# Projections of queries and keys in groups of four token tiles, their squares summed on ScalarE, and the ninth tile moved into the attention

## The chip, the cores and the metric

The kernel runs on one core of one Trainium2 chip. The metric is the device time of one execution in microseconds, the median of three runs. Engines are named as the profile names them: PE is TensorE's matmul stream and PEld its weight loads, DVE is VectorE, ACT is ScalarE, POOL is GpSimd, SP is SyncE, which issues the DMAs here (its queue is SPq).

## The reference

One inference step of one decoder layer for 1024 prompt tokens and 32 sample tokens (8 sequences of 4), width 1024. Three residual sub-layers: a mixer with two parallel branches, a cross-attention into 256 memory tokens, and a gated feed-forward network. The change touches the mixer alone:

```python
u, v, cq, ckv, kpe = split_in(rms_norm(xp, g_mix) @ w_in)     # 512, 512, 256, 256, 32 columns
a_out = gelu(u) * chunk_gmlp(v)                                # branch A, chunks of 128 tokens
ckv_n = rms_norm(ckv, g_kv_a)                                  # also an output
q = rms_norm((rms_norm(cq, g_q_a) @ w_uq), g_qk_q)             # 8 heads x 96, norm per head, rope on 32
k = rms_norm(concat([ckv_n @ w_uk, kpe]), g_qk_k)              # 8 heads x (64 + 32), norm per head, rope
vv = ckv_n @ w_uv                                              # 8 heads x 64
b_out = softmax(causal(q @ k.T * 96**-0.5)) @ vv               # branch B
xp = xp + concat([rms_norm(a_out), rms_norm(b_out)]) @ w_o
```

The sample tokens go through the same projections, but attend over 4096 cached tokens each, read from pages.

## The kernel before

Tokens are cut into nine tiles: eight of 128 prompt tokens and a ninth of the 32 sample tokens. For the projections from the input they are also cut into three chunks (`CH`) of 384, 384 and 288 tokens. Every large product is made of three matmuls (`mm3`, line 186) over operands that are split into a rounded high part (ACT, lines 192 and 196) and the rest as a low part (DVE, lines 193 and 199).

Order of the work: outside of the stretches marked `manual_schedule` the framework orders each engine's instructions by a planner of its own; inside them the listed engines keep the order of the program. Pools are regions of SBUF. All tiles of one tag in a pool share that tag's slots, and a tile waits for the tiles whose memory it takes over.

`phase1` loads the transposed input in six raw tiles of the tag `xr` (three chunks, two halves of the rows), written by `xload` on SP in program order, and splits them into `xh` and `xl`. The rows of x, needed for the squares that give each token's scale `rs_tok`, come by `tload`: tiles 0 to 2 into `xt`, tiles 3 to 8 into the memory of `a_all`, a later result, which takes over the memory of the raw tiles' pool `px`. The first product, with `w_v0`, is evacuated from five PSUM banks (`mm`) by a GELU with that scale (line 426). Further products give branch A in `a_all`. Then the chunk loop (line 506) makes the latents: cq into `cqh`, `cql`, ckv into `ckr`; sums of squares by matmuls with ones (`tok_sums`), an inverse square root on DVE of 13 small instructions (`rsqrt`, lines 221 to 232), the scale spread over the partitions by `tok_bc` (a diagonal matrix on DVE, line 275, and a matmul), the scaling (line 543), and the split into `ckh`, `ckl`. Behind each chunk `mix` normalises, transposes and stores two tiles of branch A: tiles 0 to 3, 4 to 7, and 8 behind the last chunk.

`phase2a` makes the rope tables (line 574, DVE), and for the first four heads (`hf` 0) projects q, k and v in `proj_group`, in groups of two tiles and the ninth alone. `part` evacuates q with a copy, squares it on ACT in one pass (line 791) and sums per head on DVE (line 792); for k it squares head by head with ACT's accumulator (line 789). `norm` makes the inverse square roots of a group, turns the rope part of q on POOL (lines 562 to 565), and scales k on DVE (814) and POOL (815). `head_prep` transposes a head's q and k (line 838). The second half's weights are loaded and split by `proj_weights`.

Then comes the attention, in a manual schedule: units of a head and two query tiles, 32 in order, worked off in 82 steps. Other work is put into the steps by hand, in `extra`, with `spread(fs, t0, t1)`: transposes of later heads, the second half's projections (`late`), and from step 41 on the preparation of the sample tokens. The stages behind (pages, output projection, memory attention, feed-forward network) are not touched.

Of the kernel before, what the change touches and what calls it, by code (L numbers as in the profile page):

```python
# [155 lines left out]
class Net:  # L156
# [111 lines left out]
    def tok_bc(self, p, ps, r, c):  # L268

        nc = self.nc  # L270
        o, n = CH[c]
        for i, (t0, tn) in enumerate(TILES):
            if o <= t0 < o + n:
                dg = self.t(p, [P, P], F32, "diag", 2)[:tn, :tn]
                nc.vector.tensor_scalar(dg, self.ident[:tn, :tn], r[:tn, i : i + 1], None, ALU.mult)
                nc.tensor.matmul(ps[:, t0 - o : t0 - o + tn], self.ones[:tn], dg, start=True, stop=True)


    def phase1(self):
# [25 lines left out]
        def xload(c, e):  # L305
            o, n = CH[c]
            xrs.append(self.t(px, [P, 4, 384], F32, "xr", 6)[:, :, :n])
            nc.sync.dma_start(xrs[-1], I["xT"][:, 4 * e : 4 * e + 4, o : o + n])
# [197 lines left out]
        for c, (o, n) in enumerate(CH):  # L506
# [31 lines left out]
            nc.vector.tensor_copy(self.sq_tok[:, ct], t[:, :, 0])  # L538
            nc.vector.tensor_copy(ck_tok[:, ct], t[:, :, 1])
            t = self.t(pp, [P, 512], F32, "st", 3)[:, :n]  # L540
            self.tok_bc(pl, t, ck_tok, c)
# [8 lines left out]
            for i0 in ((0, 2), (4, 6), (8,))[c]:  # L550
# [16 lines left out]
    def rope_tables(self, p, cos, sin, g, name):  # L567
# [3 lines left out]
        for nm, t in (("c", cos), ("s", sin)):  # L571
            o = p[nm] if isinstance(p, dict) else self.t(p, [P, 9, 2, 16], F32, f"{name}_{nm}")
            for h in range(2):
                nc.vector.tensor_tensor(
# [5 lines left out]
    def phase2a(self):  # L580
# [50 lines left out]
        groups = ((0, 2), (2, 4), (4, 6), (6, 8), (8, 9))  # L631
        for g in groups:
# [8 lines left out]
        st.append({**heads(), **self.proj_weights((pm, [P, 512], F32, "pth", 5), 1)})  # L641
# [16 lines left out]
        for (q, _), t in zip(late, ((16, 20), (18, 23), (21, 26), (24, 29))):  # L658
            spread(q, *t)
        spread(self.head_prep(pm, pp, 4, st[1], c), 29, 33)  # L660
        spread(sum([v for _, v in late], []) + late[4][0], 28, 38)
# [5 lines left out]
        with tc.manual_schedule(engines={E.PE, E.Activation, E.DVE}):  # L667
# [15 lines left out]
            def mix(G):  # L683
# [5 lines left out]
                nt = lambda j: self.t(p, [P, 2, 4, 96], F32, "k", 4).rearrange("p m h d -> p (m h d)")[:, :512]  # L689
# [57 lines left out]
    def proj_weights(self, raws, hf):  # L747

        nc, I, s = self.nc, self.I, {}
        for nm, src, n in (("q", I["w_uq"], 384), ("v", I["w_uv"], 256)):  # L750
            hi, lo = (self.t(self.lat, [P, 2, n], FR, f"w{nm}{x}") for x in "hl")
            for k in range(2):
                raw = self.t(*raws)[:, :n]
                nc.sync.dma_start(raw, src[:, k, hf * n : hf * n + n])
                self.split(hi[:, k], lo[:, k], raw)
# [5 lines left out]
    def proj_group(self, p, pp, hf, i0, i1, s, c, tt=("tp", 4)):  # L761
# [5 lines left out]
        def alloc():  # L767
            nonlocal r, kk, q
            r = self.t(p, [P, 2, 2, 4], F32, "hr", 2)[:tn, :m]
            kk = self.t(p, [P, 2, 4, 96], F32, "k", 4)[:tn, :m] if i0 < 8 else None  # L770
            q = self.t(p, [P, 2, 4, 96], F32, "q", 4)[:tn, :m] if i0 < 8 else self.qs[:, hf * 4 : hf * 4 + 4].unsqueeze(1)

        def part(i, z):
# [12 lines left out]
            sq = self.t(p, [P, 4, n // 4], F32, f"hsq{z}")[:tn]  # L786
            if z == 1:
                for j in range(4):
# [1347 lines left out]
```

## Time and profile before

| | us |
|---|---|
| median of the three runs | 1956.38 (1953.4 to 1957.37) |
| profiled execution | 1957.17 |
| its span | 1955.4 |
| PE busy | 1875.0 |
| DVE busy | 1358.3 |
| ACT busy | 900.5 |
| POOL busy | 680.8 |

The time is a little more than the span, by what lies around the first and last instruction. A view of stretches gives for each stretch its length, then the busy time of PE, PEld, DVE, ACT and POOL with their instructions in brackets, then the granted clock of TensorE, DMA's share and GB/s. Matmuls are pipelined, so a busy PE is not PE at its peak. A row of the timeline is start, duration, engine, line, operation, out<-in with shapes, and in square brackets how long the engine had been idle and what released it; durations of neighbours overlap, so costs of a sequence are read from start to start. A row of waits is engine and line, what it waited for, the total, how often, and the longest. The page's table of slices and its groups by line were read too; the lines that matter stand in the prediction.

### The profile page before, as it was taken

How to read it: one execution, taken by the hardware profiler on the slowest of the kernel's cores; microseconds unless marked ns; L12 is line 12 of the kernel's file. 1: busy time of each engine (PE TensorE's matmuls, PEld its weight loads, DVE VectorE, ACT ScalarE, POOL GpSimd, SP SyncE). 2: the span in 40 equal slices, each digit the busy share in tenths (PEclk: the TensorE clock that was granted, in tenths of full speed). 3: DMA queues.
4: the chain of work that ended last, by engine and by line, in shares of the span. 5: the costliest groups of instructions: out<-in, count | busy, mean ns of one | idle time of the engine just before them, and what ended most of it. 6: DMA issues, size and time to landing. Idle time of an engine off the chain costs nothing.

```text
span 1955.4 us, 40099 instructions
## 1 busy us (share of the span) xinstructions
PE 1875.0 (96%) x14538; PEld 1764.2 (90%) x14538; DVE 1358.3 (69%) x2963; ACT 900.5 (46%) x1874; POOL 680.8 (35%) x789
## 2 busy tenths in 40 slices
PE   6999899999999999999999988899999999999999
PEld 6999677769888998988799978899999999999999
DVE  7756867767777766776644659888888888832421
ACT  6335667665555555555432546332333323421311
POOL 1221311003544444544032016467677775100000
PEclk9999899999999999999999999999999999999999
DMA  8102000107765566653655045122222222754642
GB/s 294 47 18 71 22 2 34 42 21 213 213 180 167 163 174 177 173 171 128 191 155 182 23 164 180 33 77 91 74 77 68 87 88 77 221 170 127 198 123 66
DMA packets 131513, 233.75 MB, mean 120 GB/s; under 512 B 20594, under 2 KB 86995, under 8 KB 131315
## 3 DMA queue, kind: packets, MB, share of 16 engines
q1 hardware_dynamic: 130450, 230.14, 38.8%
q8 instruction: 115, 1.88, 0.4%
q10 hardware_dynamic: 864, 1.05, 0.1%
q14 instruction: 84, 0.68, 0.1%
HBM read 199.46 MB, written 31.66 MB: 118 GB/s over the span
## 4 chain that ended last, share of the span: by engine, by line
PE 68%; DVE 8%; issue 5%; DMA 4%; POOL 2%; ACT 1%; SPq 1%; POOLq 0%; DVEq 0%; ACTq 0%
PE s L186 15%; PE d L186 13%; PE X L186 7%; PE b L186 6%; PE F L186 6%; PE E L186 6%; PE A L186 3%; PE o L896 2%; PE tp L883 2%; PE o L1326 1%; PE tp L186 1%; DVE mx L1277 1%; POOL S L1274 1%; PE tp L838 1%; DVE y L1846 1%
## 5 line engine op out<-in xcount | busy, mean ns | idle before, releaser
L186 PE MATMUL s<-w2h,ch 128*128 128x288 f32 (+1 forms) x1024 | 305.9, 299 | 0.0
L186 PE MATMUL s<-w2h,cl 128*128 128x288 f32 (+1 forms) x1024 | 295.1, 288 | 2.0 <-POOL cl L1213 2.0
L186 PE MATMUL s<-w2l,ch 128*128 128x288 f32 (+1 forms) x1024 | 294.6, 288 | 0.0
L186 PE MATMUL d<-a,hi 128*128 128x264 f32 x1408 | 261.5, 287 | 3.6 <-ACT a L192 2.0
L186 PEld LDWEIGHTS d<-a,hi 128*128 128x128 f32 x1408 | 220.8, 190 | 4.8 <-DVE a L193 2.5
L186 PEld LDWEIGHTS s<-w2h,ch 128*128 128x128 f32 x1024 | 192.6, 188 | 19.1 <-issue 13.6
L186 PE MATMUL d<-a,lo 128*128 128x264 f32 x704 | 201.2, 286 | 0.0
L186 PEld LDWEIGHTS s<-w2h,cl 128*128 128x128 f32 x1024 | 192.4, 188 | 2.5 <-POOL cl L1213 2.3
L186 PEld LDWEIGHTS s<-w2l,ch 128*128 128x128 f32 x1024 | 192.8, 188 | 0.0
L1256 DVE TENSOR_REDUCE ss<-sq 128x16 f32<-128x1024 f32 x128 | 155.5, 1215 | 47.0 <-ACT sq L1253 46.8
L193 DVE TENSOR_TENSOR lo<-raw,hi 128x1024 fp32r<-128x1024 f32 (+1 forms) x71 | 82.7, 1167 | 136.2 <-ACT hi L192 136.2
L192 ACT CAST hi<-raw 128x1024 fp32r<-128x1024 f32 (+1 forms) x71 | 71.0, 1000 | 185.7 <-PE d L186 157.0
L1213 POOL TENSOR_TENSOR cl<-cT,ch 128x512 fp32r<-128x512 f32 x64 | 83.5, 1304 | 166.8 <-ACT ch L1209 145.2
L186 PEld LDWEIGHTS d<-a,lo 128*128 128x128 f32 x704 | 133.9, 190 | 0.0
L1253 ACT ACTIVATE sq<-s 128x512 f32<-128x512 f32 x128 | 76.5, 598 | 91.1 <-PE s L186 91.1
L1250 ACT ACTIVATE sq<-s 128x512 f32<-128x512 f32 x128 | 76.7, 599 | 82.0 <-PE s L186 81.7
L186 PE MATMUL mm<-whi,xh 128*128 128x256 f32 (+3 forms) x288 | 84.4, 294 | 15.6 <-ACT xh L196 9.2
L1874 POOL TENSOR_TENSOR lo<-s,hi 128x1024 fp32r<-128x1024 f32 x22 | 69.1, 3139 | 45.8 <-ACT hi L1873 45.8
L186 PE MATMUL mm<-wlo,xh 128*128 128x256 f32 (+3 forms) x288 | 83.1, 291 | 0.0
L186 PE MATMUL mm<-whi,xl 128*128 128x256 f32 (+3 forms) x288 | 83.0, 292 | 0.0
L1209 ACT CAST ch<-cT 128x512 fp32r<-128x512 f32 x128 | 73.6, 629 | 4.0 <-DMA cT<-cT 4.0
L1919 ACT COPY a<-A 128x264 f32<-128x264 f32 x44 | 16.5, 376 | 121.5 <-PE A L186 112.7
(657 smaller groups left out, 6169.6 us busy)
## 6 DMA issues: line engine op xcount, KB each, us to landing
cT<-cT SPq DMA_DIRECT2D x256, 160.0 KB, 2.4
ck<-ck SPq DMA_DIRECT2D x256, 144.0 KB, 3.3
raw<-w_up SPq DMA_DIRECT2D x44, 512.0 KB, 3.6
raw<-w_down SPq DMA_DIRECT2D x32, 512.0 KB, 3.8
actd<-cv SPq DMA_DIRECT2D x44, 264.0 KB, 2.5
araw<-actd SPq DMA_DIRECT2D x44, 264.0 KB, 4.1
raw<-w_down SPq DMA_DIRECT2D x16, 384.0 KB, 3.3
res<-res SPq DMA_DIRECT2D x16, 264.0 KB, 3.0
```

Source lines behind the costliest of these rows:

```text
L186: self.nc.tensor.matmul(out, l, r, start=first and i == 0, stop=last and i == len(seq) - 1)
L192: {"act": nc.scalar.copy, "pool": nc.gpsimd.tensor_copy, "dve": nc.vector.tensor_copy}[eng](hi, src)
L193: low = lambda: nc.vector.tensor_tensor(lo, src, hi, ALU.subtract)
L838: nc.tensor.transpose(tp[:, j * P : j * P + P], s[x, g * 4 + j][:, h % 4], self.ident)
L883: nc.tensor.transpose(tp[:, z * P : z * P + P], u[e][:, jj * P : jj * P + P], self.ident)
L896: nc.tensor.matmul(u["o"][jj * 64 : jj * 64 + 64, c], s["v"][:, j + jj, h % 4], th[:, jj * 256 : jj * 256 + c.stop - c.start], start=j == ...
L1209: nc.scalar.copy(d["h"][:, k], src[k])
L1213: (nc.vector if k else nc.gpsimd).tensor_tensor(d["l"][:, k], src[k], d["h"][:, k], ALU.subtract)
L1250: nc.scalar.activation(sq[:, 0], ps[:, :, n0 : n0 + 256], AF.Square)
L1253: nc.scalar.activation(sq[:, 1], pt.rearrange("p (e d) -> p e d", e=2), AF.Square)
L1256: yield lambda: nc.vector.tensor_reduce(s["ss"][:, g0 : g0 + 2].rearrange("p e (z h) -> p z e h", z=2), sq.rearrange("p z e (h d) -> p z e ...
L1874: eng.tensor_tensor(lo, src, hi, ALU.subtract)
```

## The change

- `xload`: each of the six raw tiles gets a tag, and so a slot, of its own.
- `tok_bc`: no diagonal matrix; the scale is read as a broadcast stationary operand and the identity moves through.
- The chunk loop: the mixing of tile 8 behind the first chunk; an Exp over one column there, whose result is not used and before which the activation table of Exp is loaded.
- `rope_tables`: on POOL instead of DVE.
- `proj_group`: groups of four tiles; q's squares head by head on ACT with the accumulator, as k's; two slots instead of four for q and k, each twice as large.
- The ninth tile's group of the first half in steps 2 to 8 of the attention; the second half's weights in slots of their own, and their splits in steps 8 to 14; the second half's groups in steps 16 to 21 and 20 to 28.
- The three mixings of branch B inside the attention take their buffers from the new slots of k.

```diff
-    def tok_bc(self, p, ps, r, c):
+    def tok_bc(self, ps, r, c):
...
-                dg = self.t(p, [P, P], F32, "diag", 2)[:tn, :tn]
-                nc.vector.tensor_scalar(dg, self.ident[:tn, :tn], r[:tn, i : i + 1], None, ALU.mult)
-                nc.tensor.matmul(ps[:, t0 - o : t0 - o + tn], self.ones[:tn], dg, start=True, stop=True)
+                self.nc.tensor.matmul(
+                    ps[:, t0 - o : t0 - o + tn], r[:tn, i : i + 1].broadcast_to([tn, P]), self.ident[:tn, :tn], start=True, stop=True
+                )
...
-            xrs.append(self.t(px, [P, 4, 384], F32, "xr", 6)[:, :, :n])
+            xrs.append(self.t(px, [P, 4, 384], F32, f"xr{c}{e}")[:, :, :n])
...
             nc.vector.tensor_copy(self.sq_tok[:, ct], t[:, :, 0])
+            if c == 0:
+
+                nc.scalar.activation(self.t(pl, [P, 1], F32, "exp"), self.sq_tok[:, :1], AF.Exp, scale=0.0)
...
-            for i0 in ((0, 2), (4, 6), (8,))[c]:
+            for i0 in ((0, 2, 8), (4, 6), ())[c]:
                 mix(i0)
...
-                nc.vector.tensor_tensor(
+                nc.gpsimd.tensor_tensor(
                     o[:, :, h], t, g[:, h * 16 : h * 16 + 16].unsqueeze(1).broadcast_to([P, 9, 16]), ALU.mult
                 )
...
-        groups = ((0, 2), (2, 4), (4, 6), (6, 8), (8, 9))
-        for g in groups:
+        groups = ((0, 4), (4, 8), (8, 9))
+        for g in groups[:2]:
             for f in sum(self.proj_group(p, pp, 0, *g, st[0], c, ("mm", 5)), []):
                 f()
...
-        st.append({**heads(), **self.proj_weights((pm, [P, 512], F32, "pth", 5), 1)})
+        more = []
+        st.append({**heads(), **self.proj_weights((pm, [P, 384], F32, "w1", 4), 1, more)})
...
-        for (q, _), t in zip(late, ((16, 20), (18, 23), (21, 26), (24, 29))):
+        for (q, _), t in zip(late, ((16, 21), (20, 28))):
             spread(q, *t)
         spread(self.head_prep(pm, pp, 4, st[1], c), 29, 33)
-        spread(sum([v for _, v in late], []) + late[4][0], 28, 38)
+        spread(sum([v for _, v in late], []) + late[2][0], 28, 38)
+
+        spread(self.proj_group(p, pp, 0, *groups[2], st[0], c)[0], 2, 8)
+        spread(more, 8, 14)
...
-                nt = lambda j: self.t(p, [P, 2, 4, 96], F32, "k", 4).rearrange("p m h d -> p (m h d)")[:, :512]
+                kb = self.t(p, [P, 4, 4, 96], F32, "k", 2).rearrange("p m h d -> p (m h d)")
+                nt = lambda j: kb[:, j * 512 : j * 512 + 512]
...
-                self.split(hi[:, k], lo[:, k], raw)
+                f = lambda hi=hi[:, k], lo=lo[:, k], raw=raw: self.split(hi, lo, raw)
+                f() if later is None else later.append(f)
...
-            r = self.t(p, [P, 2, 2, 4], F32, "hr", 2)[:tn, :m]
-            kk = self.t(p, [P, 2, 4, 96], F32, "k", 4)[:tn, :m] if i0 < 8 else None
-            q = self.t(p, [P, 2, 4, 96], F32, "q", 4)[:tn, :m] if i0 < 8 else self.qs[:, hf * 4 : hf * 4 + 4].unsqueeze(1)
+            r = self.t(p, [P, 4, 2, 4], F32, "hr", 2)[:tn, :m]
+            kk = self.t(p, [P, 4, 4, 96], F32, "k", 2)[:tn, :m] if i0 < 8 else None
+            q = self.t(p, [P, 4, 4, 96], F32, "q", 2)[:tn, :m] if i0 < 8 else self.qs[:, hf * 4 : hf * 4 + 4].unsqueeze(1)
...
-            sq = self.t(p, [P, 4, n // 4], F32, f"hsq{z}")[:tn]
-            if z == 1:
-                for j in range(4):
-                    nc.scalar.activation(sq[:, j], pv[:, j], AF.Square, accum_out=r[:, e, z, j : j + 1])
-                return
-            nc.scalar.activation(sq, pv, AF.Square)
-            nc.vector.tensor_reduce(r[:, e, z], sq, AX.X, ALU.add)
+            sq = self.t(p, [P, 4, 96], F32, "hsq", 2)[:tn]
+            for j in range(4):
+                nc.scalar.activation(sq[:, j, : n // 4], pv[:, j], AF.Square, accum_out=r[:, e, z, j : j + 1])
```

More of the change, by code (lines that the diff above doesn't have):

```diff
@@ L266, in pad @@
             self.nc.gpsimd.memset(acc[:, n:], 0.0)
-    def tok_bc(self, p, ps, r, c):
-        nc = self.nc
+    def tok_bc(self, ps, r, c):
         o, n = CH[c]
@@ L538, in phase1 @@
             nc.vector.tensor_copy(self.sq_tok[:, ct], t[:, :, 0])
+            if c == 0:
+                nc.scalar.activation(self.t(pl, [P, 1], F32, "exp"), self.sq_tok[:, :1], AF.Exp, scale=0.0)
             nc.vector.tensor_copy(ck_tok[:, ct], t[:, :, 1])
             t = self.t(pp, [P, 512], F32, "st", 3)[:, :n]
-            self.tok_bc(pl, t, ck_tok, c)
+            self.tok_bc(t, ck_tok, c)
             for m in range(2):
@@ L745, in pop_value, with proj_weights @@
             fold.append((t, u["fold"]))
-    def proj_weights(self, raws, hf):
+    def proj_weights(self, raws, hf, later=None):
         nc, I, s = self.nc, self.I, {}
```

## The prediction

> **What bounds the kernel now.** I read the page's head first, then the stretches of 50 us, then the engines in time where a stretch is not full. The profiled execution took 1957.17 us around a span of 1955.4; the three timed runs have their median at 1956.38, 0.04% below it, and what I work out on the span carries over one to one.
>
> ```profile
> PE 1875.0 (96%) x14538; PEld 1764.2 (90%) x14538; DVE 1358.3 (69%) x2963; ACT 900.5 (46%) x1874; POOL 680.8 (35%) x789
> ```
> ```profile
> 0.00:50.00 50.00, 34.42 (x247) 33.35 (x248) 36.41 (x113) 33.88 (x63) 6.96 (x13) 0.93 0.85 290
> 50.00:100.00 50.00, 50.00 (x418) 48.66 (x417) 39.93 (x147) 19.28 (x43) 13.89 (x18) 1.00 0.14 44
> ...
> 150.00:200.00 50.00, 49.64 (x352) 49.25 (x351) 33.63 (x169) 28.00 (x88) 12.18 (x23) 1.00 0.20 67
> 200.00:250.00 50.00, 40.74 (x238) 33.40 (x238) 41.06 (x165) 32.79 (x113) 14.66 (x26) 0.83 0.07 21
> 250.00:300.00 50.00, 48.94 (x332) 38.81 (x332) 36.28 (x136) 34.38 (x116) 7.16 (x12) 1.00 0.01 1
> 300.00:350.00 50.00, 49.82 (x355) 38.93 (x354) 35.75 (x148) 32.99 (x94) 8.32 (x19) 1.00 0.10 33
> ```
>
> The columns after the length are the busy time of PE, PEld, DVE, ACT, POOL, then granted clock, DMA share and GB/s. PE is the bound nearly everywhere: 50.00 of 50 from 50 to 100, 49.82 from 300 to 350. Two stretches of the part that the change touches are not full, the first 50 us and 200 to 250, and in both the granted clock is under 1 as well (0.93, 0.83). So an edit is worth something if it fills one of these two holes; work put anywhere else before 440 us costs its PE time and nothing more, as long as ACT (34.38 of 50) and DVE (36.28) keep room.
>
> **Hole one: raw inputs in their own buffers.**
>
> ```profile
> 20.00:30.00 10.00, 10.00 (x87) 10.00 (x86) 8.53 (x35) 6.81 (x16) 0.00 (x0) 1.00 0.47 160
> ...
> 35.00:41.40 6.40, 0.01 (x1) 0.01 (x1) 5.67 (x22) 3.66 (x6) 1.72 (x3) 0.83 1.08 364
> 41.40:45.00 3.60, 3.60 (x17) 2.96 (x18) 3.60 (x10) 2.40 (x7) 3.60 (x6) 0.50 1.06 332
> ```
> ```profile
> PE mm L186 <- ACT gv L426: 6.4, 1, 6.4
> ```
> ```profile
> 10.57 2.44 SPq L308 DMA_DIRECT2D xr<-xT  x2
> 26.48 1.76 SPq L313 DMA_DIRECT2D a_all<-x  x4
> ```
> ```profile
> 20.64 1.05 ACT L323 ACTIVATE xt<-xt 128x1024 f32<-128x1024 f32 x1
> ...
> 30.21 1.06 ACT L323 ACTIVATE a_all<-a_all 128x1024 f32<-128x1024 f32 x1 [0.97 <-DMA a_all<-x]
> ...
> 40.86 1.20 ACT L426 ACTIVATE gv<-mm,rs_tok 128x256 f32<-128x256 f32 x3 [1.95 <-DVE rs_tok L232]
> ...
> 49.70 1.05 ACT L323 ACTIVATE a_all<-a_all 128x1024 f32<-128x1024 f32 x1
> ...
> 51.79 0.45 ACT L456 ACTIVATE a_all<-mm,rs_tok 128x256 f32<-128x256 f32 x1
> ```
> ```profile
> 25.50 0.95 DVE L199 SCALAR_TENSOR_TENSOR xl<-xr,cols,xh 128x288 fp32r<-128x288 f32 x2
> ```
>
> PE stands still for 6.4 us from 35.0, because all five mm banks wait for the GELU of tile 3, which needs that tile's row scale, hence the squares of x (30.21), hence a load that SP issued only at 26.48. SP had nothing between 13.0 and 26.48, and DMA was half idle (share 0.47). What held it is memory: the token rows are loaded into a_all, which lies on the raw tiles xr, and the load goes out right after the last read of any of them (25.50 + 0.95 = 26.45). Six tiles of one tag share six slots, in an order that the allocator chooses. With a tag each, in order of first use, the 18 KB of a_all would lie on the two raw tiles of the first chunk (6 KB each) and on the token-row buffers xt, last read at 20.64 + 1.05 = 21.7. The load then goes out 26.48 − 21.7 = 4.8 us earlier, and the chain of scales with it. PE cannot gain more than about that: next late are the squares of tiles 7 and 8 (49.70), whose end lets a_all be written (51.79) and a bank come free just as PE needs one; they hang on the same queue and move by the same amount. Bounds: 0 (the new layout still puts a_all on a raw tile read at the end), and 6.4 for the stall plus 1.8 for the 3.6 us that follow it at a clock of 0.50, so 8.2. I take 4.7. What is hidden here: no load is added, only moved into the idle DMA time.
>
> **Hole two: from the latents to the attention.**
>
> ```profile
> 194.78 0.14 DVE L533 TENSOR_TENSOR lss<-st,rs_tok 128x6 f32<-128x6 f32 x1
> ...
> 202.61 0.70 DVE L539 COPY ck_tok<-lss 128x3 f32<-128x3 f32 x1
> ...
> 210.87 0.94 DVE L543 SCALAR_TENSOR_TENSOR ckr<-ckr,cols,st 128x288 f32<-128x288 f32 x2
> ```
> ```profile
> 189.78 19.55 SPq L1483 DMA_DIRECT2D mix<-hl  x2
> ```
> ```profile
> 204.93 0.43 PE L1479 MATMUL st<-ident,csq 32*128 32x32 f32 x4
> ...
> 211.90 0.58 PE L186 MATMUL mm<-w2h,ckh 128*128 128x256 f32 x1 [2.79 <-ACT ckh L192]
> ...
> 218.10 0.33 PE L186 MATMUL mm<-wqh,cqh 128*32 128x384 f32 x1
> ...
> 219.79 0.28 PE L186 MATMUL mm<-w2h,ckl 128*32 128x256 f32 x1
> ...
> 232.74 0.61 PE L186 MATMUL s<-kTh,qTh 96*128 96x320 f32 x1
> ```
> ```profile
> 187.36 0.48 ACT L785 COPY q<-mm 128x384 f32<-128x384 f32 x1
> ...
> 190.78 0.45 ACT L785 COPY q<-mm 128x384 f32<-128x384 f32 x1
> 191.14 0.48 ACT L791 ACTIVATE hsq<-mm 128x384 f32<-128x384 f32 x1
> 191.52 0.34 ACT L785 COPY k<-mm 128x256 f32<-128x256 f32 x1
> 191.77 0.21 ACT L789 ACTIVATE hsq<-mm 128x64 f32<-128x64 f32 x1
> ...
> 192.57 0.34 ACT L781 COPY v<-mm 128x256 f32<-128x256 f32 x1
> ...
> 211.42 0.86 ACT L192 CAST ckh<-ckr 128x288 fp32r<-128x288 f32 x2 [2.18 <-DVE ckr L543]
> ...
> 221.00 0.30 ACT L789 ACTIVATE hsq<-mm 128x64 f32<-128x64 f32 x1
> ```
>
> The last chunk's latents go through a chain on DVE that takes from 194.78 to 210.87, 16 us, although its own instructions are some 20 like the first row (0.14) and two of 0.5. DVE's queue has between them the rope tables, the reductions of q, the norms of three groups, the ninth tile's mixing and the diagonals. PE waits 2.79 us for the result and runs at half clock behind it. The last squares of keys end at 221.30; then come the norm, the scaling of k, the transposes and, at 232.74, the first scores of the third unit, after which PE stays full.
>
> What the edits take out of DVE here: the reductions of q, eight rope-table instructions and the last chunk's three diagonals, the 13 of the norm of tile 8's mixing, and three of five group norms; the rope tables go to POOL. I do not add up DVE, since its bubble disappears into the next bound, ACT. A tile on ACT now takes, start to start from the rows, 0.36 for the copy of q, 0.38 for its squares, 0.25 for the copy of k, 0.80 for its four squares (191.77 to 192.57, 0.20 each) and 0.26 for v, the same 256 columns as k. Afterwards q too takes four squares; a pass of 96 columns instead of 64 adds 32 columns at (0.36 − 0.25)/128 us, so 0.23 each and 0.92 for 0.38. A tile is then 2.59 us, eight are 20.7, and from 187.36, with four casts of the latents (two take 0.86) in between, the last squares end at 187.36 + 20.7 + 1.7 = 209.8 instead of 221.30. PE needs less: twelve matmuls for q and k of a tile start within 219.79 − 218.10 = 1.7 us, so 1.8 in all, and v adds six. I take 11 of these 11.5, the rest for lock-step over five banks. Behind the last squares the 11.4 us to the scores stay: the ninth tile's norm and the splits of the second half's weights leave DVE's queue there, but k is scaled for four tiles at a time, by DVE and by POOL, so that part doubles. Bounds: 15 (those 11.4 lose the ninth tile's norm and the four subtractions, at most 13 × 0.15 and 4 × 0.5, an estimate of 4 us, and the doubling costs nothing), and 4, which is what is left if the chain of the last chunk keeps half of its 16 us and the ninth tile's 1.8 us alone go. Three edits lie inside this bound and get no term. tok_bc keeps its nine matmuls, with the roles of the operands exchanged. The early Exp brings one table load forward, from the first exponential of the attention to a stretch where ACT is busy 28.00 of 50. And SP, whose queue stood 19.55 us at the store of the ninth tile's mixing with the second half's weights behind it, is free earlier, but those are wanted only at step 16 of the attention.
>
> **What is paid later.** The ninth tile's q and k go into the attention's steps 2 to 8, where PE is full: 1.8 us on the path. Its mixing goes to the first chunk, also full: four small transposes, 0.4 (204.93). The splits of the weights (four casts, four subtractions) and its norm go to ACT and DVE in the attention, at nothing: the cover is the room of 15 us in 50 that both have there. The second half's q squares put 8 × 0.54 = 4.3 us more on ACT and take eight reductions from DVE; at nothing, by the same cover. The upper end: three parts are now issued in a step where two were, and if PE waits out what ACT needs more for a part, (2.59 − 0.26)/2 = 1.17 against 0.9, in all 16, that is 4.3.
>
> Sum: −4.7 − 11 + 1.8 + 0.4 = −13.5 us, 1957.17 → 1943.7, or 1942.9 on the median's scale.
>
> **Rule against row.** POOL's new tables and its ropes, now four tiles wide, run beside DVE's short chains.
>
> ```profile
> 197.26 0.77 POOL L562 TENSOR_TENSOR rp<-q,tq_c 128x256 f32<-128x256 f32 x1
> ...
> 199.24 0.47 POOL L565 TENSOR_TENSOR q<-rp,rp 128x128 f32<-128x128 f32 x1
> ```
> ```profile
> 197.12 0.16 DVE L229 TENSOR_TENSOR rqa<-rqy 128x16 f32<-128x16 f32 x1
> ...
> 197.35 0.71 DVE L230 TENSOR_TENSOR rqa<-rqa,rqh 128x16 f32<-128x16 f32 x1
> ```
>
> A product of 16 columns took 0.16 just before POOL's instruction began and 0.71 beside it, and both ended within 0.03 us (197.26 + 0.77, 197.35 + 0.71). [...]
>
> For hole one, the row of 41.40 shows a clock of 0.50 behind an idle of 6.4 us. [...]
>
> **Rivals.** (1) The raw buffers do nothing: a_all still lies on a tile that is read last, since the order of slots is not in the profile. For it: nothing but the time of 26.45 ties the load to xr. Then −8.8 remains, 1947.6 on the median's scale. (2) POOL holds the chains: for the second group the ropes of q take twice what two tiles take from 197.26 to 199.24 + 0.47, 4.9 us, beside the last norm, and if DVE waits for all of it hole two gives 6.1 instead of 11: −8.6, 1947.8. [...] (3) The slower side: ACT becomes the bound in the attention. Ahead of every exponential stand now three parts with eight to twelve squares; ACT pays 4.3 us for q, 2.1 for the ninth tile (0.36 + 0.92 + 0.80) and 1.2 for the splits (at the price of the copies), PE 2.2. If PE waits for all of it, that is 9.8, and it decides only where the two holes give less than that together; with hole one at 0 and hole two at its lower bound of 4 the kernel is 6 us slower, 1962. Against it: ACT has 34.38 of 50 there, 4.3 us more over 45 us leaves it under 80%.
>
> **How the numbers follow.** Both holes shrink as worked out: 0.60. One of them does not (rivals 1 and 2): 0.22. Slower: 0.08. No change that can be told, which here means within 0.2% or 3.9 us, because ACT pays back what the holes give: 0.07. Better than the bounds: 0.03. Faster is 0.60 + 0.22 + 0.03 = 0.85. The time is that of the likeliest, 1942.9. The range's lower end takes both upper bounds, −8.2 − 15 + 2.2 = −21, 1935; the upper end is that of rivals 1 and 2 with the 4.3 us of ACT's excess, rounded up, 1953.
>
> **What would show it.** Hole one: SP's loads of a_all near 21.7, and no wait of PE for gv above 2 us; wrong if they go out at 26 again. Hole two: L543 of the last chunk before 202, the last squares of keys near 210 less 4.7, and the third unit's first scores near 217; wrong if PE still waits for ckh. Attention: the first scores of the third unit to the end of the last unit 2 us longer than before, with no wait of PE for pr or pth above 1 us; wrong if PE waits for exponentials in steps 16 to 25. All later stages should be shifted and otherwise the same.

## The result and the profile after

The changed kernel takes 1965.07 us (median of seven runs, 1962.31 to 1971.2) against 1956.38 for the kernel before: a ratio of 1.0054, 95% interval 1.0037 to 1.0072. It is slower by half a per cent, where 1942.9 us and a gain were predicted. Line numbers from the chunk loop on are shifted by two to five (543 became 545, 791 became 796, 866 became 870). The profiled execution is the median one, with a span of 1963.4 us, 8.0 more than before.

First the page's busy times and the view of stretches, with the columns as before.

```profile
PE 1878.7 (96%) x14538; PEld 1767.4 (90%) x14538; DVE 1343.0 (68%) x2856; ACT 910.0 (46%) x2001; POOL 682.7 (35%) x777
```
```profile
0.00:50.00 50.00, 35.03 (x264) 33.73 (x265) 38.18 (x117) 35.33 (x67) 7.44 (x13) 0.93 0.86 292
200.00:250.00 50.00, 43.33 (x266) 36.51 (x264) 35.65 (x122) 33.10 (x136) 13.71 (x20) 0.86 0.07 20
250.00:300.00 50.00, 44.51 (x271) 35.40 (x270) 30.09 (x102) 32.23 (x131) 6.04 (x5) 0.90 0.00 1
300.00:350.00 50.00, 48.99 (x347) 38.07 (x345) 31.42 (x118) 35.83 (x135) 8.81 (x14) 1.00 0.10 33
```

DVE has 15 us less work and ACT 10 more, as the edits say. The stretch from 200 us has PE busier by 2.6 us; the one from 250 us, full before at a clock of 1.00, has lost 4.4 us and shows 0.90. The waits of PE up to 235 us, and those from 235 to 320 us (total, how often, longest):

```profile
PE mm L186 <- ACT gv L425: 5.8, 1, 5.8
PE tp L842 <- POOL k L819: 5.5, 1, 5.5
PE st L273 <- DVE ck_tok L541: 1.5, 1, 1.5
```
```profile
PE s L186 <- DVE pr L870: 5.5, 2, 4.1
```

The wait for gv is there still, the one for ckh is gone, one for k of 5.5 us is new, and in the attention PE waits twice for pr, the evacuated scores; there it stood for 1.0 us before. To follow the loss I read three marks in the timeline of each run: the last input matmul (on xh), and the small matmuls of `cmr` and `idr` that put the causal mask on a block of scores, 64 of them up to some 430 us, in the same order in every kernel.

| from, to | before | after | difference |
|---|---|---|---|
| start to the last input matmul | 185.90 | 185.06 | −0.8 |
| to the fifth mask matmul (third unit) | 48.31 | 43.48 | −4.8 |
| fifth to tenth (ninth tile's q and k) | 11.31 | 13.15 | +1.8 |
| tenth to 19th (splits of the weights) | 26.77 | 29.68 | +2.9 |
| 19th to 31st (second half's q and k) | 51.91 | 59.30 | +7.4 |
| 31st to 64th | 98.56 | 98.61 | +0.1 |

That makes 6.5 of the 8.0 us; the other 1.5 come behind the attention and were not followed (that part, the same code in every run told of here, takes 1528.9 to 1536.5 us in their profiles, so 1.5 us there say nothing). The rows behind each difference, from the timelines of the changed kernel, first phase one:

```profile
21.66 2.92 SPq L312 DMA_DIRECT2D a_all<-x  x4
29.00 1.04 ACT L322 ACTIVATE a_all<-a_all 128x1024 f32<-128x1024 f32 x1
35.51 1.22 DVE L193 TENSOR_TENSOR wlo<-wraw,whi 128x1024 fp32r<-128x1024 f32 x1
36.92 1.75 DVE L193 TENSOR_TENSOR wlo<-wraw,whi 128x1024 fp32r<-128x1024 f32 x1
38.60 0.68 DVE L232 SCALAR_TENSOR_TENSOR rs_tok<-rqa,rqy 128x3 f32<-128x3 f32 x1
39.37 1.20 ACT L425 ACTIVATE gv<-mm,rs_tok 128x256 f32<-128x256 f32 x3 [2.94 <-DVE rs_tok L232]
```

The loads go out at 21.66 instead of 26.48, but the first square comes at 29.00 instead of 30.21: it stands behind other work in ACT's queue. Then two wide low parts stand among the small steps of rs_tok on DVE. PE goes on at 39.90, 1.5 us earlier than before.

Not even that is a gain that can be told. Ten of the kernels below share phase one with the changed kernel. In these eleven PE's wait for gv lies between 5.6 and 8.6 us and the last input matmul between 185.06 and 189.07, with 186.45 in the middle; the kernel before has 6.4 and 185.90. What differs most among them is when POOL comes. In the kernel before its products of gv wait for another load; with the loads of x earlier they start sooner and stand beside the steps of rs_tok on DVE (first the kernel before, then the run with the later norm):

```profile
39.69 2.44 POOL L439 TENSOR_TENSOR gv<-gv,rows 128x256 f32<-128x256 f32 x3 [38.67 <-DMA rows<-rows]
```
```profile
35.26 2.33 POOL L438 TENSOR_TENSOR gv<-gv,rows 128x256 f32<-128x256 f32 x3 [34.24 <-DVE gv L436]
36.25 0.68 DVE L229 TENSOR_TENSOR rqa<-rqy 128x3 f32<-128x3 f32 x1
```

The last nine steps of this rs_tok, 0.16 us each when nothing holds them, take 1.9 to 2.0 us together in the kernel before and in the profile of the changed kernel, 3.0 in six of the other ten and 4.5 to 4.8 in four, whose waits for gv are the longest (7.1 to 8.6 us).

```profile
193.36 0.17 DVE L532 TENSOR_TENSOR lss<-st,rs_tok 128x6 f32<-128x6 f32 x1 [1.70 <-PE st L260]
195.12 0.42 DVE L224 TENSOR_SCALAR rqy<-rqy 128x6 int32<-128x6 int32 x1
200.87 0.93 DVE L545 SCALAR_TENSOR_TENSOR ckr<-ckr,cols,st 128x288 f32<-128x288 f32 x2
201.40 0.86 ACT L192 CAST ckh<-ckr 128x288 fp32r<-128x288 f32 x2 [2.95 <-DVE ckr L545]
212.47 0.48 ACT L796 ACTIVATE hsq<-mm 128x64 f32<-128x64 f32 x1
217.04 2.10 POOL L819 TENSOR_TENSOR k<-kr,hr 128x512 f32<-128x512 f32 x1 [3.20 <-DVE hr L232]
219.21 1.09 PE L842 MATMUL tp<-ident,k 128*96 128x128 f32 x4 [5.45 <-POOL k L819]
227.21 0.61 PE L186 MATMUL s<-kTh,qTh 96*128 96x320 f32 x1
```

Ahead of the attention the last chunk's chain ends at 200.87 instead of 210.87, yet ACT stands idle 2.95 us for it, the last squares end at 212.95, and the norm and scaling of four tiles take from there to 219.14. The third unit's first scores come at 227.21 (before 232.74).

```profile
252.08 0.54 DVE L193 TENSOR_TENSOR wql<-w,wqh 128x384 fp32r<-128x384 f32 x1
253.40 0.56 DVE L193 TENSOR_TENSOR wql<-w,wqh 128x384 fp32r<-128x384 f32 x1 [0.78 <-ACT wqh L192]
254.43 0.44 PE L186 MATMUL s<-kTh,qTh 96*128 96x384 f32 x1 [1.43 <-DVE pr L870]
```
```profile
284.11 0.41 DVE L801 TENSOR_TENSOR hr<-hr,sq_tok 128x16 f32<-128x16 f32 x1 [3.15 <-ACT hsq L796]
284.55 1.21 DVE L802 TENSOR_TENSOR hr<-hr,sq_tok 128x16 f32<-128x16 f32 x1
289.49 0.47 DVE L870 TENSOR_SCALAR_CACHE_REDUCE pr<-s 128x320 f32<-128x320 f32 x1
290.03 0.69 PE L186 MATMUL s<-kTh,qTh 96*128 96x384 f32 x1 [4.06 <-DVE pr L870]
```

Twice DVE, which keeps the program's order here, waits for ACT ahead of a score evacuation: 0.78 us for a cast of a weight, and 3.15 us for the squares of tiles 0 to 3, behind which 13 steps of their norm follow, and a low part, before pr has its turn at 289.49. PE waits 1.43 and 4.06 us. The stretches of 5 us around the second place:

```profile
278.00:283.00 5.00, 5.00 (x35) 4.18 (x34) 1.21 (x4) 4.83 (x34) 0.00 (x0) 1.00 0.01 2
288.00:293.00 5.00, 2.97 (x11) 2.40 (x11) 3.73 (x16) 0.00 (x0) 0.00 (x0) 0.65 0.01 3
293.00:298.00 5.00, 5.00 (x24) 4.16 (x21) 3.45 (x13) 2.28 (x11) 2.11 (x1) 0.67 0.00 0
```

ACT is busy 4.83 of 5 us ahead of the stall and has nothing to do from 288 on, and the granted clock is 0.65 and 0.67 in the two stretches from there.

### The profile page after: what moved, and what is told of

It reads as the page before. It is cut to its first block, busy times and chain, and to the rows that moved or that the text cites. A ratio compares the mean times of both kernels' runs of the same rounds, so it can differ in the third digit from the quotient of the medians.

```text
span 1963.4 us, 40098 instructions
## 1 busy us (share of the span) xinstructions
PE 1878.7 (96%) x14538; PEld 1767.4 (90%) x14538; DVE 1343.0 (68%) x2856; ACT 910.0 (46%) x2001; POOL 682.7 (35%) x777
## 3 DMA queue, kind: packets, MB, share of 16 engines
q10 hardware_dynamic: 864, 1.05, 0.1%
## 4 chain that ended last, share of the span: by engine, by line
PE 77%; DVE 10%; DMA 4%; issue 4%; ACT 2%; POOL 2%; SPq 1%; DVEq 0%; POOLq 0%; ACTq 0%
PE s L186 15%; PE d L186 13%; PE mm L186 7%; PE b L186 7%; PE X L186 6%; PE F L186 6%; PE E L186 6%; PE A L186 3%; PE o L900 2%; PE tp L887 2%; PE tp L186 1%; PE o L1330 1%; DMA araw<-actd 1%; DMA ck<-ck 1%; PE tp L842 1%
```

## The experiments

Theory A held that the loss in the attention is the place of the norm and of the low parts in DVE's queue; its rival B, that ACT simply has too much to do there. Each run's ratio is to the kernel before on the same chip. It tells some 0.15% apart, 3 us, so single stages are compared by the marks above. The start of the attention moves by up to 4 us between kernels whose phase one is the same (last input matmul at 185.06 to 189.07); stages are therefore counted from that matmul on. The stage behind it is not steady either: in the changed kernel and the four runs that differ from it only inside the attention (norm later, sum on DVE, pairs, two parts to a step) the fifth mask matmul comes 40.65 to 45.05 us behind the last input matmul. All five are ahead of the 48.31 of the kernel before, but a difference of less than 4 us between two of them says nothing by itself. The marks inside the attention are steadier: 19th to 31st takes 58.9 to 59.3 us in the four profiles that have there what the changed kernel has.

**Only the norm of tiles 0 to 3 later.**

```diff
-        for (q, _), t in zip(late, ((16, 21), (20, 28))):
-            spread(q, *t)
+        spread(late[0][0][:9], 16, 19)
+        spread(late[0][0][9:], 21, 24)
+        spread(late[1][0], 20, 28)
```

> Against the changed kernel only the six norm steps of tiles 0 to 3 of the second half stand elsewhere: in steps 21 to 23 of the attention in place of steps 19 and 20; the squares on ScalarE stay where they are, three parts a step. Theory A (VectorE's queue: the norm that waits for ScalarE's backlog of squares stands ahead of score evacuations): TensorE's wait of 4.06 us for pr near 290 us is under 1 us, the half clock of 288 to 298 us is gone, and the attention ends 5 to 7 us earlier: ratio to the kernel before 1.001 to 1.003. Rival B (ScalarE has too much work there, exponentials come late): ScalarE's load is the same, the wait stays above 3 us or is taken over by a wait for pth or pr of the same length, ratio 1.005 to 1.006.

Ratio 1.0054 (1.0034 to 1.0073); 19th to 31st mask matmul 56.07 us, in place of 59.30. Theory A alone is not enough: 3.2 of the 7.4 us come back and 4.2 stay. PE's longest wait for pr is 2.1 us now. In DVE's timeline its cause has another name; ACT is full for 10 us ahead of it, and so it is in the changed kernel if both are counted from their 19th mask matmul (this run is 4.6 us later there):

```profile
291.43 0.75 DVE L199 SCALAR_TENSOR_TENSOR qTl<-tp,ggq,qTh 96x512 fp32r<-96x512 f32 x1 [5.87 <-ACT qTh L196]
```
```profile
278.00:283.00 5.00, 5.00 (x37) 4.36 (x35) 0.00 (x0) 4.94 (x31) 0.00 (x0) 1.00 0.00 0
283.00:288.00 5.00, 5.00 (x35) 4.14 (x33) 1.20 (x4) 4.83 (x35) 0.19 (x1) 1.00 0.01 2
```

DVE now idles for ACT's evacuation of transposed queries, which stands behind the squares of eight parts in ACT's queue. That is B's mechanism.

**The second half's queries squared in one pass, summed on DVE.**

```diff
+            if z == 0 and hf == 1 and i < 8:
+                nc.scalar.activation(sq, pv, AF.Square)
+                nc.vector.tensor_reduce(r[:, e, z], sq, AX.X, ALU.add)
+                return
```

> Against the changed kernel the squares of the second half's queries alone are made by one ScalarE instruction of 384 columns and summed by one on VectorE, as in the kernel before; the groups of four and all places stay. ScalarE loses some 8 x 1 us, VectorE gains some 8 x 0.5 us. Theory A: the norm still waits for the last of the parts, but the backlog of ScalarE is shorter, so the wait of 4.06 us shrinks to 1 to 2 us: ratio 1.002 to 1.004. Rival B: ScalarE's count was the cause, the wait is gone and all of the 7 us are back: 1.001 to 1.002. If the place of the norm alone decides, and not the count, nothing changes: 1.005.

Ratio 1.0049 (1.0034 to 1.0063), 19th to 31st 59.36 us, PE's longest wait for pr 4.1 us again: the last of the three expected cases. ACT was busy 28.60 instead of 32.23 us between 250 and 300 us, and nothing came back: with the norm in this place ACT's total is not what counts. The edit also gives DVE eight sums that wait for ACT.

**The second half's weights split on POOL.**

```diff
-                f = lambda hi=hi[:, k], lo=lo[:, k], raw=raw: self.split(hi, lo, raw)
-                f() if later is None else later.append(f)
+                if later is None:
+                    self.split(hi[:, k], lo[:, k], raw)
+                else:
+                    later.append(lambda hi=hi[:, k], raw=raw: nc.gpsimd.tensor_copy(hi, raw))
+                    later.append(lambda hi=hi[:, k], lo=lo[:, k], raw=raw: nc.gpsimd.tensor_tensor(lo, raw, hi, ALU.subtract))
```

> Against the changed kernel the casts and low parts of the second half's weights, at the same steps of the attention, go to GpSimd. Theory A: the 2.9 us that the attention loses between its 13th and 15th unit (low parts on VectorE wait for ScalarE's cast, and a score evacuation stands behind them) come back, the 7 us at the norm of tiles 0 to 3 stay: ratio 1.0035 to 1.0045. Rival C: those 2.9 us are ScalarE's or TensorE's (the ninth tile's share, a late exponential): the loss stays, ratio 1.005 to 1.006. GpSimd's slower passes over 128x384 may hold VectorE instead: then above 1.006.

Tenth to 19th mask matmul 26.76 us, in place of 29.68 and equal to before: the 2.9 us are the splits' (1.35 where the clock does not fall, see the last section). The ratio, 1.0061 (1.0036 to 1.0085), does not show it: POOL is not one of the engines under the manual schedule, and the planner put the four splits of the v weights among its ropes ahead of the attention (216.28 to 219.8), where the fifth mask matmul came 48.51 us behind the last input matmul instead of 43.48 (1.6 us of it in PE's wait for k, 7.1 instead of 5.5).

**The second half's tiles 0 to 7 in pairs,** by a `norm` that takes a pair of the group of four:

```diff
-        for (q, _), t in zip(late, ((16, 21), (20, 28))):
-            spread(q, *t)
+        pairs = [x for g in late[:2] for x in g[0]]
+        for q, t in zip(pairs, ((16, 20), (18, 23), (21, 26), (24, 29))):
+            spread(q, *t)
```

> Against the changed kernel the second half's tiles 0 to 7 are normed in pairs at the kernel before's steps (16 to 20, 18 to 23, 21 to 26, 24 to 29); the squares stay on ScalarE, four instructions each with its sum. Theory A: a pair's norm waits for two tiles' squares, not four, at two parts a step and not three, so that ScalarE has no backlog: the 7 us come back wholly, 1.001 to 1.003. Rival B (ScalarE's count of squares): the count is the same, so at least half of the loss stays, 1.003 to 1.006.

Ratio 1.0004 (0.9990 to 1.0018), 19th to 31st 51.61 us: all of the 7.4 is back with every square still on ACT. Pairs change two things, though: the norm is half as wide, and the parts stand two to a step, not three.

**Groups of four, two parts to a step, norm later.**

```diff
-        for (q, _), t in zip(late, ((16, 21), (20, 28))):
-            spread(q, *t)
+        spread(late[0][0][:9], 16, 20)
+        spread(late[0][0][9:], 21, 24)
+        spread(late[1][0], 20, 28)
```

> Against the changed kernel the eight projections with squares of tiles 0 to 3 of the second half stand two to a step in steps 16 to 19 of the attention (three to a step in 17 and 18 before), and their norm, of all four tiles at once as in the changed kernel, in steps 21 to 23. Two theories after the last runs, in which the later norm alone gave back little and pairs gave back nearly all. D (density: ScalarE's queue takes three parts a step, some 2.6 us a tile, ahead of copies and exponentials that TensorE needs): the stall of TensorE near 290 us is under 1.5 us and the attention from its first to its last mask matmul takes 197 to 199 us, as with pairs (197.65), against 206.3 in the changed kernel; ratio 1.000 to 1.002. E (size: a norm of four tiles, 32 columns, holds VectorE's or GpSimd's queue too long wherever it stands): the attention stays at 202 us or more, ratio 1.003 or more.

Ratio 1.0010 (0.9993 to 1.0026), 19th to 31st 52.47 us, first to 64th 197.59. Against the first experiment only the eight parts are spread over four steps instead of three, and 3.6 us more come back. The same stretches as above, and PE's waits from 235 to 320 us:

```profile
278.00:283.00 5.00, 5.00 (x39) 4.45 (x38) 0.72 (x2) 4.97 (x28) 0.25 (x1) 1.00 0.00 2
283.00:288.00 5.00, 4.73 (x30) 3.92 (x29) 3.75 (x15) 3.26 (x25) 3.70 (x4) 1.00 0.02 3
288.00:293.00 5.00, 5.00 (x33) 4.10 (x31) 4.49 (x21) 5.00 (x26) 0.00 (x0) 1.00 0.00 0
```
```profile
PE s L186 <- DVE pr L871: 1.7, 2, 1.4
```

ACT is nearly as full (9.4 of the 10 us that begin 5 us behind the 19th mask matmul, 9.8 in the first experiment), but PE runs through at a clock of 1.00. So in this order of edits the 7.4 us come apart: 3.2 for the norm's place right behind the parts, 3.6 for three parts in a step, 0.6 left against the kernel before (0.9 against the pairs) for the size of the group. The two costs are not independent: in the pairs, at two parts to a step, the norm also stands right behind its parts and costs nothing.

One cause is hidden in the 3.2. In the changed kernel four steps of the norm took 0.41, 1.21, 0.69 and 0.65 us; they stand beside POOL's rope of the same tiles. In this run POOL idles when they come, and the same four take 0.17 or 0.18 (one row of each, the changed kernel first):

```profile
284.44 1.28 POOL L565 TENSOR_TENSOR rp<-q,tq_s 128x512 f32<-128x512 f32 x1
```
```profile
290.38 0.17 DVE L803 TENSOR_TENSOR hr<-hr,sq_tok 128x16 f32<-128x16 f32 x1
```

By these rows some 2.3 of PE's 4.06 us are POOL's, an estimate; no run takes that rope away in the attention.

**The raw buffers alone,** on the kernel before (the `xr` line of the change).

> Against the kernel before only the raw inputs get buffers of their own. The prediction had 4.7 us less by it (ratio 0.9976), its rival nothing (1.000). By the trace of the changed kernel: the loads of a_all go out near 21.7 us in place of 26.48, but TensorE's wait for gv shrinks by less than 1 us and the whole by 0.8 to 1.5 us: ratio 0.9992 to 0.9996. Its own profile tells between them: wait for gv 5.5 to 6.4 us, or 1.7.

Ratio 1.0002 (0.9989 to 1.0016). The loads went out at 22.14, PE's wait for gv was 5.6 us instead of 6.4, the last input matmul stood at 185.66 instead of 185.90. The buffers alone gain nothing that can be told.

**The weights u of the first half split later.**

```diff
-            wu = wsplit(f"u{hf}")
+            if hf:
+                wu = wsplit("u1")
...
                     squares(pg, i0, i0 + 3)
+                    if i0 == 3:
+                        wu = wsplit("u0")
```

> Against the changed kernel the weights u of the first half are split after the squares of token tiles 3 to 5, not ahead of them. If what holds gv is the low parts of these weights (1.22 and 1.75 us) that stand on VectorE among the steps of rs_tok, TensorE's wait for gv falls from 5.8 us to 2.5 to 4 us and the stages behind start 2 to 3 us earlier: ratio 1.004 against 1.0054. If the landing of a_all (or of x) holds it, the wait stays at 5.5 us or more. If the later split is then itself missing for the matmuls that use it, a new wait for wlo or whi of 2 us or more appears there and nothing is won.

Inconclusive: 1.0051 (1.0031 to 1.0072), wait 5.6 us. The planner put the low parts ahead of the end of rs_tok all the same (35.48 and 37.91), so the edit did not move what it was to move.

**The low parts of u left out,** with copies by ACT in their place.

```diff
+                if name == "u0":
+                    nc.scalar.copy(hi[:, k : k + 4], raw[:, k : k + 4])
+                    nc.scalar.copy(lo[:, k : k + 4], raw[:, k : k + 4])
+                    continue
```

> Against the changed kernel the low parts of the first half's weights u are not computed: ScalarE, which idles there, writes a second copy of the weights in their place, so VectorE loses two instructions of 1.22 and 1.75 us. If these two, standing among the steps of rs_tok on VectorE, hold gv, TensorE's wait for gv falls from 5.8 us to 2.8 to 3.6 us and the last input matmul from 185.06 to 182.5 to 183; ratio about 1.004. If the wait is set by the squares or by the twelve steps of rs_tok alone, it stays above 5 us.

Ratio 1.0031 (1.0019 to 1.0042).

```profile
37.88 0.42 PE L186 MATMUL mm<-whi,xh 128*32 128x256 f32 x1 [3.94 <-ACT gv L429]
```

The wait falls from 5.76 to 3.94 us and the last input matmul comes at 183.50, in place of 185.06. The two instructions hold up to 1.8 us, a little less than expected: 0.5 of it is the last step of rs_tok, 0.16 us here and 0.68 beside POOL in the changed kernel. The rest of the wait is the squares and the steps themselves.

**The first half's tiles 4 to 7 in pairs.**

```diff
-            for f in sum(self.proj_group(p, pp, 0, *g, st[0], c, ("mm", 5)), []):
+            q, v = self.proj_group(p, pp, 0, *g, st[0], c, ("mm", 5), pairs=g[0] == 4)
+            for f in (sum(q, []) if g[0] == 4 else q) + v:
                 f()
```

> Against the changed kernel tiles 4 to 7 of the first half, ahead of the attention, are normed in two pairs; all else stays. If the chain behind the last squares is long because it is four tiles wide (norm on 32 columns, k scaled on VectorE 1.22 us and GpSimd 2.10 us side by side, all four k transposes behind it), the time from the last squares (212.6 in the changed kernel) to the third unit's first scores (228.5), 15.9 us, falls to 12 to 14 us, TensorE's wait for k from 5.5 us to 3 to 4 us: ratio 1.004. If the width does not matter, the order of ScalarE's queue does, and both numbers stay within 0.7 us.

From the end of the last squares to the fifth mask matmul 12.51 us, where the changed kernel has 15.59 (13.8 to 16.0 in the seven profiles with groups of four and no splits on POOL) and the kernel before 12.91; PE's wait for k is 1.0 us, where those seven have 5.5. So the width of four does cost something behind the last squares, 1.3 to 3.5 us. What is left of it from the last input matmul on cannot be told: 41.13 us instead of 43.48, inside the 40.65 to 45.05 of runs with the same code up to there. The ratio, 1.0053 (1.0035 to 1.0071), is too coarse for it. (The 228.5 that the expectation calls the third unit's first scores is its mask matmul; the first scores stand at 227.21.)

**Three edits together** (pairs in the second half, splits on POOL, pairs for tiles 4 to 7 of the first half), **and the same with the low parts of u on POOL.**

> The changed kernel with three edits together: the second half's tiles 0 to 7 in pairs at the kernel before's steps, the second half's weights split on GpSimd, tiles 4 to 7 of the first half normed in pairs. If the losses found are separate, the attention from its first to its last mask matmul takes 195 us (26.8 from the 10th to the 19th mask matmul and 51.6 from there to the 31st) and starts 5.2 to 7.5 us earlier than in the kernel before: ratio 0.996 to 0.998, the first version that is faster than both. If they share a cause, or GpSimd's splits collide with the pairs, 0.999 to 1.002.

> As the version with three edits, and the low parts of the first half's weights u on GpSimd, with the right values. If VectorE's two instructions hold gv, another 1 to 2.4 us: ratio 0.995 to 0.997. If GpSimd's passes over 128x1024 (2.4 us each or more) hold VectorE's steps of rs_tok, or delay GpSimd's products of gv that stand behind, nothing or a loss of up to 2 us: 0.997 to 0.999.

Three edits: 0.9993 (0.9982 to 1.0003), tenth to 19th 26.77, 19th to 31st 51.62: the attention's losses are separate, and only the ninth tile's 1.7 us stay. The ratio is nevertheless that of the second case, since ahead of the attention the gain is 4.9 us: less than the expected 5.2 to 7.5, and far from the 11 of the prediction. With u on POOL: 0.9997 (0.9981 to 1.0013); PE waited 8.7 us for gv, so POOL makes that hole longer: its two low parts take 4.74 us together, and two steps of rs_tok beside them 2.31 and 2.27. That is neither of the two expected ratios.

**The last chunk's chain.** In the version with three edits the same stall is plainer:

```profile
199.23 0.17 DVE L536 TENSOR_TENSOR lss<-lss,rs_tok 128x6 f32<-128x6 f32 x1
199.31 1.24 DVE L808 TENSOR_TENSOR hr<-hr,sq_tok 128x16 f32<-128x16 f32 x1
200.54 1.23 DVE L541 COPY ck_tok<-lss 128x3 f32<-128x3 f32 x1
199.23 1.29 POOL L564 TENSOR_TENSOR rp<-q,tq_c 128x512 f32<-128x512 f32 x1
200.48 1.27 POOL L565 TENSOR_TENSOR rp<-q,tq_s 128x512 f32<-128x512 f32 x1
201.83 1.78 PE L273 MATMUL st<-ident,ck_tok 128*128 128x128 f32 x6 [3.02 <-DVE ck_tok L541]
```

A copy of three columns takes 1.23 us beside POOL's rope pass. Two runs on that version, the first without the rope of the first half's queries of tiles 0 to 3 (it is left out), the second with the tables on DVE:

```diff
-            self.rope_tok(p, q_[:, :, :, 64:], q_[:, :, :, 64:], [t[:tn, j0:j1] for t in c["qt"]], 4, tn, m)
+            if hf or i0:
+                self.rope_tok(p, q_[:, :, :, 64:], q_[:, :, :, 64:], [t[:tn, j0:j1] for t in c["qt"]], 4, tn, m)
```
```diff
-                nc.gpsimd.tensor_tensor(
+                nc.vector.tensor_tensor(
                     o[:, :, h], t, g[:, h * 16 : h * 16 + 16].unsqueeze(1).broadcast_to([P, 9, 16]), ALU.mult
```

> Against the version with three edits, the rotation of the first half's queries of tiles 0 to 3 on GpSimd is left out (two passes of 1.3 us over 128x512 and two of 0.75 us), nothing else. Theory F (GpSimd's passes hold VectorE's small steps in the chain of the last chunk: there a copy of three columns took 1.23 us on VectorE beside such a pass, and 0.15 without one): the copy to ck_tok is at 199.3 to 199.8 in place of 200.54, TensorE's wait for ck_tok falls from 3.0 us to 0.5 to 1.2 us, and the scaling of the last chunk's latents comes at 201 to 201.5 in place of 203.65. Rival G (the chain is just as long for VectorE's own queue): all three stay within 0.5 us.

> The version with three edits, with the rope tables made on VectorE again, as in the kernel before. VectorE was idle for 2.4 us ahead of the chain of the last chunk and has room for part of the eight tables; GpSimd's rotations then start some 3.5 us earlier and run out of the way of the chain's end. By theory F TensorE's wait for ck_tok falls from 3.0 to 1 to 2 us and the attention starts 1 to 2 us earlier: ratio 0.998 to 0.999. If the tables land among the chain's steps instead, 1 us is lost and the ratio is 0.999 to 1.000.

Without the rope (0.9988, 0.9974 to 1.0002), the copy and PE's wait:

```profile
200.81 0.16 DVE L541 COPY ck_tok<-lss 128x3 f32<-128x3 f32 x1
201.03 1.04 PE L273 MATMUL st<-ident,ck_tok 128*128 128x128 f32 x6 [1.18 <-DVE ck_tok L541]
```

Its last input matmul came 1.0 us later (186.86 against 185.85), so the copy's place is to be taken from there: it ends 14.1 us behind that matmul in place of 15.9, the scaling of the latents starts at 15.25 in place of 17.80, and the fifth mask matmul at 39.67 in place of 43.38. Theory F stands for the steps: two that took 1.24 and 1.23 us beside POOL take 0.17 and 0.16, 2.1 of the 2.5 us by which the scaling is earlier. The 3.7 us up to the third unit lie within what that stage varies by. How much the passes cost is chance: in the twelve profiles of the new order that have them on POOL the scaling comes 14.9 to 18.0 us behind the last input matmul, according to which steps they meet. With the tables on DVE nothing is won (0.9997, 0.9982 to 1.0012; scaling at 17.47): the same two passes merely met two other steps of the chain, which took 1.13 and 1.19 us.

**That rope on DVE, nothing left out.**

```diff
-            self.rope_tok(p, q_[:, :, :, 64:], q_[:, :, :, 64:], [t[:tn, j0:j1] for t in c["qt"]], 4, tn, m)
+            self.rope_tok(p, q_[:, :, :, 64:], q_[:, :, :, 64:], [t[:tn, j0:j1] for t in c["qt"]], 4, tn, m, None if hf or i0 else nc.vector)
```

> The version with three edits, with the rotation of the first half's queries of tiles 0 to 3 on VectorE in place of GpSimd; nothing is left out. In VectorE's order its two wide passes stand behind the copy to ck_tok, where VectorE waits 1.5 us for TensorE anyway. By theory F TensorE's wait for ck_tok falls from 3.0 us to about 1.2 us, as without the rotation, the last chunk's latents are scaled 15.3 to 16 us after the last input matmul (17.8 in the version with three edits), and the attention starts 2 to 3.5 us earlier: ratio 0.997 to 0.9985. If VectorE's added 1.9 us delay the scaling by as much as GpSimd's passes did, nothing changes: 0.999 to 1.000.

1950.11 us against 1956.05 of the kernel before: 0.9977 (0.9966 to 0.9989), the one version that beats both kernels; against the version with three edits (0.9993, 0.9982 to 1.0003) the intervals touch.

```profile
200.20 0.16 DVE L541 COPY ck_tok<-lss 128x3 f32<-128x3 f32 x1
200.41 1.04 PE L273 MATMUL st<-ident,ck_tok 128*128 128x128 f32 x6 [1.00 <-DVE ck_tok L541]
200.44 0.69 DVE L564 TENSOR_TENSOR rp<-q,tq_c 128x512 f32<-128x512 f32 x1
```

The rope takes 0.69 a pass on DVE and stands behind the copy, where DVE would wait for PE. The scaling comes 15.28 us behind the last input matmul, as without the rope. The fifth mask matmul comes at 41.49, 1.9 us earlier and not 3.7: PE then waits 2.1 us for k, which DVE scales.

## Why the prediction failed

It said −13.5 us and got +8.7 by the medians. By its own terms:

- **Hole one, −4.7: mis-sized, −0.8 in this profile and no gain over all runs** (1.0002 alone). The loads went out at 21.7 as said. The step that failed let everything behind them move with them. ACT's queue ate 3.6 of the 4.8 us up to the first square, DVE's order holds gv for another 1.8 at most, and POOL's products, now earlier too, stand beside the steps of rs_tok in most runs, the last nine of which take 3.0 to 4.8 us in ten profiles, not 1.9 to 2.0. Rival 1 had the size, nothing, and not the reason: a_all did leave the late raw tiles.
- **Hole two, −11: mis-sized, −4.7** at the third unit's first scores, beyond the −0.8 of hole one (by the fifth mask matmul −3.3 to −7.7 in the five profiles with this code). ACT's price of 2.59 us a tile held (2.32 from one copy of q to the next without v's 0.26, and the four squares of k 0.20 each as before), and the chain ended before 202 as said. But the bound took ACT for a queue that never waits: it idled 2.95 and 0.42 us for the last chunk. And the 11.4 us behind the last squares became 14.3; the doubled width was named there and priced at nothing net. These two make the 6.3 us that are missing. Rival 2, POOL on the chains, was no rival but a part of this term, with 2.1 to 2.5 us in the chain of the version with three edits, and by the rows it acts in hole one (0.68 us for the last step of rs_tok, 0.16 in the run without the low parts of u) and in the attention's norm (an estimate of 2.3 us) as well.
- **Ninth tile, +1.8: right,** 1.84. The 0.4 for the mixing was not seen by itself.
- **Splits in the attention, 0: +2.9,** of which 1.35 without the fall of the clock. The cover was called the room of ACT and DVE. Room in a stretch is no cover in a queue in program order: the low part waits for a cast, and a score evacuation waits behind it.
- **Second half's squares and groups, 0 with 4.3 as upper end: +7.4,** above the upper end. That bound counted what ACT has to do more. The cost was ACT's burst of three parts a step and a norm that waits for its last square ahead of pr and is then held by POOL's rope. Rival 3 had that place (steps 16 to 25) and the backlog on ACT, but put the wait on the exponentials; it came through DVE.

The losses stood where the prediction put zeros, and the range had no end for them: it let the attention cost at most 4.3 us more.

## What to carry to other kernels

Where engines keep the program's order, price a moved step by what stands right behind it in each queue and by the wait that it brings along; a busy share says nothing on that. Work put into steps by hand wants a rate that the slowest queue clears within a step, and its consumer some steps later. When a load comes earlier, follow the chain to the next queue before counting the gain, and look at what else it sets free: here POOL's products, beside which the steps of rs_tok took longer (its last nine 3.0 to 4.8 us in ten profiles, in place of 1.9 to 2.0). And before a stage of one profile is compared with that of another, see how far it varies between runs with the same code.

## What the runs showed of the hardware

The same wait of PE cost different amounts. In the changed kernel 1.43 us of idling for pr at 254.43 was followed by half the clock (0.50 from 256 to 258 us); in the run with the later split of u, 1.44 us at the same matmul was not (stretch 254 to 258 us, the changed kernel first):

```profile
254.00:258.00 4.00, 3.57 (x16) 2.57 (x17) 3.08 (x13) 0.00 (x0) 0.00 (x0) 0.67 0.00 0
```
```profile
254.00:258.00 4.00, 3.24 (x22) 2.70 (x23) 3.33 (x14) 0.73 (x3) 0.00 (x0) 1.00 0.00 0
```

With the fall, tenth to 19th took 29.6 to 29.7 us (the changed kernel and five of the runs told of here), without it 28.1 (two runs). So the length of the wait, 1.43 against 1.44 us, did not decide by itself whether the clock fell; what did was not shown. In this kernel a wait under 2 us could therefore not be counted on to be followed by full clock.

In the version with three edits two of DVE's steps took 1.24 and 1.23 us beside POOL's passes of 1.29 and 1.27, and each ended within 0.03 us of its pass; with the passes left out they took 0.17 and 0.16. POOL's work was longer beside DVE's as well: the two scalings of k, which start within 0.05 us of each other, took 1.05 us on POOL and 2.08 on DVE in the first group of the changed kernel, 2.10 and 1.22 in the second. That one of them stood behind the other there is the author's reading of these four times.
